# Matmul with layer norm: row pieces of A laid out for contiguous transposes, and a last row tile in six column ranges

## The chip, the cores and the metric

The kernel runs on one core of a Trainium2 chip. The metric is the time of one execution on the device in microseconds (us). Eight runs of the kernel before gave a median of 252.48 us, from 251.8 to 254.12.

The core has five engines that run side by side[...]: TensorE (PE in the profile; its weight loads are PEld), VectorE (DVE), ScalarE (ACT), GpSimd (POOL) and SyncE (SP). SP, ACT and POOL also issue transfers between memory (HBM) and the on-chip memory SBUF. TensorE writes its products to PSUM, eight banks of 512 fp32 columns on 128 partitions.

## The reference

```python
x = np.matmul(a, b)                         # a, b: 2048 x 2048, fp32
mean = np.mean(x, axis=-1, keepdims=True)
var = np.var(x, axis=-1, keepdims=True)
normalized = (x - mean) / np.sqrt(var + eps)
return (gamma * normalized + beta).astype(np.float32)
```

A product of two square matrices, and each row of it normalised to mean 0 and variance 1, scaled by gamma and shifted by beta. The inputs are cast to fp16 for the product; sums, statistics and output are fp32.

## The kernel before

**Tiles.** The 2048 rows of the output are 16 row tiles of 128. A row tile's 2048 columns are four banks of 512 (`bank`, L128), and each bank is the sum of 16 matmuls over the inner dimension (`mm`, L131). B stays on the chip in fp16 as `b16`, 16 slices of 128 inner rows. `b_rows` (L65) deals the inner index as `(c p t)` with t = 4, so that slice 4c + t holds inner index 512 c + 4 p + t on partition p; A's transposes use the same order.

**First four row tiles.** They run while B is still loading (L233 to L362): rows of A come in 16 pieces (`load_first`), VectorE casts them, TensorE turns them (`turn_first`, L99), VectorE keeps them (`keep_first`). Their products are made in two halves of the inner dimension, the first half put aside by ScalarE (`put_by`) and added later by VectorE (`add_up`).

**Later row tiles, 4 to 15.** Each comes in two halves h of the inner dimension. `load_tile` (L108) issues four transfers for a half, one for each group of 32 partitions; SP issues those of tiles 4 and 5, POOL those of tiles 6 to 15, into four buffers ("first"). In `a_pieces` (L66) partition r of group q holds rows 4 r + j, j = 0 to 3, of the row tile, for columns 512 c + 128 q to + 127. ScalarE casts a half (`cast_tile`, L114), 1024 elements a partition. VectorE then turns 32 x 32 blocks (`transpose_part`, L122): one call takes one j, all four c, 512 elements a partition; it reads inner index k in steps of 4 elements and writes rows r into `at` in steps of 4 elements.

**Order.** The engines' orders are those of the program text (L215 to L219): every engine executes its instructions in the order in which the Python code emits them, and the framework adds the semaphores. The loop over row tiles 4 to 15 (L370) emits for tile i: the normalisation of tile i - 1 (`normalise`, L179), then for each bank its 16 matmuls, its statistics on VectorE (`stats`, L137) and, up to i = 13, a cast and a transpose for tile i + 2. For i from 4 to 11 half a normalisation of one of the first four tiles follows as well (L384).

**Normalising.** `aggregate` (L151) joins four statistics into mean and variance on VectorE and takes the square root of variance + eps on ScalarE; `invert` (L159) is VectorE's reciprocal. Each bank is centred and multiplied by gamma (`centre`, L164, which reads PSUM and so frees the bank), then multiplied by the reciprocal and added to beta (`scale`, L170). SP sends out halves of 1024 columns.

**The last row tile** has its own normalisation (`normalise_last`, L194): after the last bank's statistics VectorE does three of the banks, each centred and scaled, and ScalarE and POOL do the fourth; four output transfers of 512 columns follow, three from SP and one from ScalarE's queue.

Of the kernel before, what the change touches and what calls it, by code (L numbers as in the profile page):

```python
# [9 lines left out]
FP32 = mybir.dt.float32  # L10
FP16 = mybir.dt.float16
AluOp = mybir.AluOpType
ActFn = mybir.ActivationFunctionType

@with_exitstack
def kernel(
# [18 lines left out]
    nc = tc.nc  # L35
    P = 128
    M, K = a.shape
    _, N = b.shape
    n_mt = M // P
    n_kt = K // P  # L40
    NB = 512
    n_nb = N // NB
    NH = N // 2
    G = 4

    konst = ctx.enter_context(tc.tile_pool(name="konst", bufs=1))
    bpool = ctx.enter_context(tc.tile_pool(name="bpool", bufs=1))
    bigp = ctx.enter_context(tc.tile_pool(name="bigp", bufs=8))
    firstp = ctx.enter_context(tc.tile_pool(name="firstp", bufs=4))
# [3 lines left out]
    xpool = ctx.enter_context(tc.tile_pool(name="xpool", bufs=16))  # L53
    upool = ctx.enter_context(tc.tile_pool(name="upool", bufs=2))
    stat = ctx.enter_context(tc.tile_pool(name="stat", bufs=6))
    psum = ctx.enter_context(tc.tile_pool(name="psum", bufs=1, space=bass.MemoryType.PSUM))

    gamma_b = konst.tile([P, N], FP32)
    beta_b = konst.tile([P, N], FP32)
    eps_t = konst.tile([P, 1], FP32)  # L60
    warm = konst.tile([P, NB], FP16)
    ident = konst.tile([P, P], FP16)
    b16 = bpool.tile([P, n_kt, N], FP16)

    b_rows = b.rearrange("(c p t) n -> c t p n", p=P, t=4)  # L65
    a_pieces = a.rearrange("(i r j) (c q k) -> q i r (j c) k", r=32, j=4, c=4, q=4)  # L66

    bnst, x_of, mv_of, rs_of, at = {}, {}, {}, {}, {}
    a_in, b_in, t_of, tile_in, part = {}, {}, {}, {}, {}
# [36 lines left out]
        nc.vector.tensor_copy(at[g][:, ds(4 * c, 4), :], t_of[n])  # L106

    def load_tile(i, h, queue):  # L108
        f = firstp.tile([P, 8, P], FP32, tag="first", name=f"p{i}_{h}")
        for q in range(4):  # L110
            queue.dma_start(f[ds(32 * q, 32)], a_pieces[q, i][:, ds(8 * h, 8)])  # L111
        tile_in[i, h] = f

    def cast_tile(i, h):  # L114
        a16 = a16p.tile([P, 2, 4, P], FP16, tag="a16", name=f"a{i}_{h}")
        nc.scalar.copy(a16.rearrange("p j c k -> p (j c) k"), tile_in.pop((i, h)))  # L116
        tile_in[i, h] = a16

    def new_at(i):
        at[i] = atp.tile([P, n_kt, P], FP16, tag="at", name=f"at{i}")  # L120

    def transpose_part(i, j):  # L122
        nc.vector.transpose(  # L123
            at[i].rearrange("p ct (r j) -> p j ct r", j=4)[:, j],
            tile_in[i, j // 2][:, j % 2].rearrange("p c (k t) -> p c t k", t=4),
        )

    def bank(i, q):  # L128
        x_of[i, q] = psum.tile([P, NB], FP32, tag="c_ps", bufs=8, name=f"ps_{i}_{q}")

    def mm(i, q, kt, lo=0, hi=n_kt):  # L131
        nc.tensor.matmul(  # L132
            x_of[i, q], at[i][:, kt, :], b16[:, kt, ds(q * NB, NB)],
            start=(kt == lo), stop=(kt == hi - 1),
        )

    def stats(i, q):  # L137
        if i not in bnst:
            bnst[i] = stat.tile([P, n_nb, 6], FP32, tag="bnst", name=f"bnst{i}")
        nc.vector.bn_stats(bnst[i][:, q, :], x_of[i, q])  # L140
# [10 lines left out]
    def aggregate(i):  # L151
        mv = stat.tile([P, 2], FP32, tag="mv", name=f"mv{i}")
        nc.vector.bn_aggr(mv, bnst[i])  # L153
        sq = stat.tile([P, 1], FP32, tag="sq", name=f"sq{i}")
        nc.scalar.activation(sq, mv[:, 1:2], ActFn.Sqrt, bias=eps_t)  # L155
        mv_of[i] = mv
        return sq

    def invert(i, sq):  # L159
        rs = stat.tile([P, 1], FP32, tag="rs", name=f"rs{i}")  # L160
        nc.vector.reciprocal(rs, sq)  # L161
        rs_of[i] = rs

    def centre(i, q, u):  # L164
        nc.vector.scalar_tensor_tensor(  # L165
            u, x_of[i, q], mv_of[i][:, 0:1], gamma_b[:, ds(q * NB, NB)],
            AluOp.subtract, AluOp.mult,
        )

    def scale(i, q, u, c):  # L170
        nc.vector.scalar_tensor_tensor(  # L171
            c[:, ds(q % 2 * NB, NB)], u, rs_of[i], beta_b[:, ds(q * NB, NB)],
            AluOp.mult, AluOp.add,
        )

    def new_c(i, h):
        return bigp.tile([P, NH], FP32, tag="big", name=f"c{i}_{h}")

    def normalise(i, h=None):  # L179
        if h in (None, 0):  # L180
            sq = aggregate(i)
        for half in (0, 1) if h is None else (h,):
            c = new_c(i, half)
            us = []
            for q in (2 * half, 2 * half + 1):
                us.append(upool.tile([P, NB], FP32, tag="u", name=f"u_{i}_{q}"))
                centre(i, q, us[-1])
                if q == 0:
                    invert(i, sq)
            for q in (2 * half, 2 * half + 1):  # L190
                scale(i, q, us[q % 2], c)
            nc.sync.dma_start(out[ts(i, P), ds(half * NH, NH)], c)

    def normalise_last(i):  # L194
        sq = aggregate(i)
        c = [new_c(i, 0), new_c(i, 1)]
        centre(i, 0, x_of[i, 0])
        invert(i, sq)
        shift = stat.tile([P, 1], FP32, tag="shift", name="shift")
        nc.vector.scalar_tensor_tensor(  # L200
            shift, mv_of[i][:, 0:1], -1.0, rs_of[i], AluOp.mult, AluOp.mult)
        q3 = ds(3 * NB, NB)
        y = upool.tile([P, NB], FP32, tag="u", name="y_last")
        nc.scalar.activation(y, x_of[i, 3], ActFn.Identity, bias=shift, scale=rs_of[i])  # L204
        nc.gpsimd.tensor_tensor(y, y, gamma_b[:, q3], AluOp.mult)  # L205
        nc.gpsimd.tensor_tensor(c[1][:, NB:NH], y, beta_b[:, q3], AluOp.add)
        for q in range(3):
            if q:
                centre(i, q, x_of[i, q])
            scale(i, q, x_of[i, q], c[q // 2])  # L210
            nc.sync.dma_start(
                out[ts(i, P), ds(q * NB, NB)], c[q // 2][:, ds(q % 2 * NB, NB)])
        nc.scalar.dma_start(out[ts(i, P), q3], c[1][:, NB:NH])

    order = {  # L215
        mybir.EngineType.PE, mybir.EngineType.DVE, mybir.EngineType.Activation,
# [2 lines left out]
    with tc.manual_schedule(engines=order):  # L219
# [5 lines left out]
        def warm_up(n):  # L225
# [4 lines left out]
            out=ident, in_=ident, compare_op=AluOp.not_equal, fill=1.0,  # L230
# [17 lines left out]
        for i in (4, 5):  # L248
            for h in (0, 1):
                load_tile(i, h, nc.sync)  # L250
        nc.sync.dma_start(gamma_b, gamma.unsqueeze(0).to_broadcast([P, N]))
        nc.sync.dma_start(beta_b, beta.unsqueeze(0).to_broadcast([P, N]))
        for i in range(6, n_mt):
            for h in (0, 1):
                load_tile(i, h, nc.gpsimd)
# [13 lines left out]
        for n in range(KH):  # L269
            g, c = pieces[n]  # L270
# [34 lines left out]
        for t in range(KH):  # L305
            n = KH + t
# [47 lines left out]
        for h in (0, 1):  # L354
            cast_tile(4, h)
            transpose_part(4, 2 * h)
            transpose_part(4, 2 * h + 1)
# [7 lines left out]
        for c in range(4):  # L365
            if c % 2 == 0:
                cast_tile(5, c // 2)
            transpose_part(5, c)

        for i in range(G, n_mt):  # L370
            if i > G:
                normalise(i - 1)
            if i + 2 < n_mt:
                new_at(i + 2)
            for q in range(n_nb):
                bank(i, q)
                for t in range(n_kt):
                    mm(i, q, t)
                stats(i, q)
                if i + 2 < n_mt:  # L380
                    if q % 2 == 0:
                        cast_tile(i + 2, q // 2)
                    transpose_part(i + 2, q)
                if q == 3 and i < 3 * G:  # L384
                    normalise((i - G) // 2, (i - G) % 2)
        normalise_last(n_mt - 1)

_INS = ['a', 'b', 'gamma', 'beta', 'eps']
_OUTS = [((2048, 2048), 'float32')]
# [28 lines left out]
```

## Time and profile before

| | us |
|---|---|
| median of 8 runs | 252.48 |
| the profiled execution | 252.12 |
| its span, first to last instruction | 250.3 |
| TensorE busy | 233.7 (93%) |
| VectorE busy | 213.9 (85%) |
| ScalarE busy | 58.4 (23%) |
| POOL busy | 49.2 (20%) |
| transposes on VectorE (L123), 48 | 61.4 |
| POOL's transfers of A (L111), 80 of 128 KB | 46.2 |
| TensorE waiting for centring (L165) | 3.6 |

The span is the time between the first and last instruction that the profiler saw; the execution takes a little longer. A group's duration counts from an instruction's start to its end, and neighbouring instructions of one engine overlap by some of it, so that the distance between two starts is the better price of one more instruction in a row. In a line of the order of time the first number is the start, the second the length of the merged stretch, xN the number of instructions in it, and the bracket, where there is one, is how long the engine had been idle and what ended this.

### The profile page before, as it was taken

Reading aid. Unit: us, or ns where it says so; the run is one execution under the profiler, and the core shown is the slowest. Engines: PE = TensorE matmul, PEld = TensorE weight load, DVE = VectorE, ACT = ScalarE, POOL = GpSimd, SP = SyncE. Lnnn points to the kernel's source line nnn. Section 1 sums busy time; section 2 is a strip of 40 time slices with the busy share of each in tenths; the row PEclk is TensorE's granted clock in tenths of the full one; section 3 lists DMA queues with packets and bytes.
Section 4 is the critical chain, followed back from the end, with each engine's and each line's share of the span. In section 5 each row is a group of like instructions: output and inputs, shape, how many; then the busy total and the mean of one; then the engine's idle time right before and its main releaser. Section 6 shows DMA issues by size and latency. Waiting matters only on the chain.

```text
span 250.3 us, 3093 instructions
## 1 busy us (share of the span) xinstructions
PE 233.7 (93%) x1108; PEld 106.4 (42%) x1108; DVE 213.9 (85%) x354; ACT 58.4 (23%) x91; POOL 49.2 (20%) x87
## 2 busy tenths in 40 slices
PE   7999999999999999999999999989979899999940
PEld 2444454444444444444444444434434344444410
DVE  1654454379999999999999999999999999999953
ACT  2225728641511321030300303011030303000010
POOL 0000000000732907051160702407042000000003
PEclk9999999999999999999999999999999999999996
DMA  5999999999999837458272762908448240404214
GB/s 183 404 394 403 402 401 408 408 367 169 226 283 230 208 91 235 147 191 230 86 233 102 239 180 106 310 25 230 169 153 264 90 168 3 168 0 168 115 53 168
DMA packets 20302, 52.62 MB, mean 210 GB/s; under 512 B 2880, under 2 KB 6976, under 8 KB 20032
## 3 DMA queue, kind: packets, MB, share of 16 engines
q1 hardware_dynamic: 16160, 41.16, 45.9%
q0 software_dynamic: 3840, 10.49, 16.9%
q10 hardware_dynamic: 288, 0.79, 0.9%
q8 instruction: 8, 0.13, 0.3%
q14 instruction: 6, 0.05, 0.1%
HBM read 35.65 MB, written 16.78 MB: 209 GB/s over the span
## 4 chain that ended last, share of the span: by engine, by line
DVE 56%; PE 28%; DMA 8%; issue 3%; ACT 2%; SPq 0%; DVEq 0%
PE ps L132 27%; DVE at L123 19%; DVE c L171 12%; DVE u L165 10%; DVE bnst L140 9%; DMA f<-in_a_dram 5%; DMA w<-in_b_dram 3%; DVE x L148 2%; ACT x L144 2%; DVE ps L165 1%; PE t_ps L102 1%; DVE mv L153 1%; ACT b L84 1%; DVE b L83 1%; DVE rs L161 1%
## 5 line engine op out<-in xcount | busy, mean ns | idle before, releaser
L132 PE MATMUL ps<-b,at 128*128 128x512 f16 x1024 | 224.4, 379 | 4.0 <-DVE u L165 3.6
L132 PEld LDWEIGHTS <-at 128*128 128x128 f16 x1024 | 99.7, 98 | 123.3 <-issue 5.9
L111 POOL DMA_DIRECT2D p<-in_a_dram x80 | 46.2, 585 | 141.7 <-DMA p<-in_a_dram 70.5
L123 DVE STREAM_TRANSPOSE at<-a 128x512 f16<-128x512 f16 x48 | 61.4, 1303 | 0.0
L171 DVE SCALAR_TENSOR_TENSOR c<-u,rs,beta_b 128x512 f32<-128x512 f32 x60 | 42.1, 744 | 0.0
L155 ACT ACTIVATE sq<-mv,eps_t 128x1 f32<-128x1 f32 x16 | 4.7, 295 | 136.2 <-DVE mv L153 136.2
L140 DVE BATCH_NORM_STATS2 bnst<-ps 128x6 f32<-128x512 f32 x48 | 30.9, 653 | 2.4 <-PE ps L132 2.4
L165 DVE SCALAR_TENSOR_TENSOR u<-ps,mv,gamma_b 128x512 f32<-128x512 f32 x44 | 31.6, 742 | 0.4
L116 ACT CAST a<-p 128x1024 f16<-128x1024 f32 x24 | 24.1, 1037 | 15.5 <-DMA p<-in_a_dram 15.5
L96 DVE CAST h<-f 128x512 f16<-128x512 f32 x16 | 6.8, 423 | 9.3 <-DMA f<-in_a_dram 9.3
L78 DVE CAST b<-w 128x512 f16<-128x512 f32 x16 | 6.7, 425 | 9.2 <-DMA w<-in_b_dram 9.2
L79 ACT CAST b<-w 128x512 f16<-128x512 f32 x16 | 9.6, 619 | 17.2 <-DMA w<-in_b_dram 17.2
L84 ACT CAST b<-w 128x512 f16<-128x512 f32 x16 | 10.0, 624 | 14.3 <-DMA w<-in_b_dram 14.3
L148 DVE TENSOR_TENSOR x<-ps,x 128x512 f32<-128x512 f32 x16 | 10.4, 683 | 3.1 <-PE ps L132 2.9
L205 POOL TENSOR_TENSOR y_last<-y_last,gamma_b 128x512 f32<-128x512 f32 x1 | 1.3, 1260 | 54.2 <-ACT y_last L204 54.2
L165 DVE SCALAR_TENSOR_TENSOR u<-x,mv,gamma_b 128x512 f32<-128x512 f32 x16 | 11.3, 727 | 0.2
L106 DVE COPY at<-t_ps 128x512 f16<-128x512 f16 x16 | 6.7, 421 | 4.7 <-PE t_ps L102 4.6
L140 DVE BATCH_NORM_STATS2 bnst<-x 128x6 f32<-128x512 f32 x16 | 10.0, 679 | 0.0
L227 PE MATMUL w_ps<-warm 128*128 128x512 f16 x20 | 7.4, 514 | 1.2 <-DVE warm L220 1.2
L144 ACT COPY x<-ps 128x512 f32<-128x512 f32 x16 | 8.4, 611 | 0.1
L83 DVE CAST b<-w 128x512 f16<-128x512 f32 x16 | 6.7, 417 | 2.0 <-DMA w<-in_b_dram 2.0
L102 PEld LDWEIGHTS <-h 128*128 128x128 f16 x64 | 5.3, 115 | 6.9 <-DVE h L96 2.8
(19 smaller groups left out, 25.3 us busy)
## 6 DMA issues: line engine op xcount, KB each, us to landing
w<-in_b_dram SPq DMA_DIRECT2D x31, 512.0 KB, 8.5
out_dram<-c SPq DMA_DIRECT2D x30, 512.0 KB, 2.7
p<-in_a_dram POOLq DMA_DIRECT2D x80, 128.0 KB, 5.4
f<-in_a_dram SPq DMA_DIRECT2D x16, 256.0 KB, 7.2
p<-in_a_dram SPq DMA_DIRECT2D x16, 128.0 KB, 5.2
gamma_b<-in_gamma_dram SPq DMA_DIRECT2D x1, 1024.0 KB, 10.0
beta_b<-in_beta_dram SPq DMA_DIRECT2D x1, 1024.0 KB, 14.9
out_dram<-c SPq DMA_DIRECT2D x3, 256.0 KB, 2.5
```

The source lines that it names most:

```text
L79: nc.scalar.copy(b16[:, kt, NB:NH], w[:, NB:NH])
L83: nc.vector.tensor_copy(b16[:, kt, NH:NH + NB], w[:, 0:NB])
L84: nc.scalar.copy(b16[:, kt, NH + NB:N], w[:, NB:NH])
L111: queue.dma_start(f[ds(32 * q, 32)], a_pieces[q, i][:, ds(8 * h, 8)])
L116: nc.scalar.copy(a16.rearrange("p j c k -> p (j c) k"), tile_in.pop((i, h)))
L123: nc.vector.transpose(at[i].rearrange("p ct (r j) -> p j ct r", j=4)[:, j], tile_in[i, j // 2][:, j % 2].rearrange("p c (k t) -> p c t k", ...
L132: nc.tensor.matmul(x_of[i, q], at[i][:, kt, :], b16[:, kt, ds(q * NB, NB)], start=(kt == lo), stop=(kt == hi - 1),)
L140: nc.vector.bn_stats(bnst[i][:, q, :], x_of[i, q])
L144: nc.scalar.copy(part[i, q], x_of[i, q])
L148: nc.vector.tensor_tensor(x, x_of[i, q], x, AluOp.add)
L165: nc.vector.scalar_tensor_tensor(u, x_of[i, q], mv_of[i][:, 0:1], gamma_b[:, ds(q * NB, NB)], AluOp.subtract, AluOp.mult,)
L171: nc.vector.scalar_tensor_tensor(c[:, ds(q % 2 * NB, NB)], u, rs_of[i], beta_b[:, ds(q * NB, NB)], AluOp.mult, AluOp.add,)
```

## The change

**Layout of tiles 4 to 15.** Partition r of a group now holds rows r, 32 + r, 64 + r and 96 + r of the row tile (32 s + r, with s = 0 to 3). A half's transfers are issued for one c at a time: eight of 64 KB, each of 32 partitions x 4 rows x 512 bytes, in place of four of 128 KB. One call of `transpose_part` now takes one c and all four j; it reads as before in steps of 4 elements and writes rows r of `at` next to each other.

**Mean of the last row tile by a matmul.** `b16` grows by 32 columns. In tiles 6 to 13 ScalarE sums every half row of B (`sum_b`, 32 calls of 1024 elements, the copy itself going to `junk`). After tile 14's matmuls and statistics, `mean_b` makes from these the mean of each row of B on VectorE, splits it into two fp16 parts, and ScalarE copies them into columns 2048 and 2049 of each of the 16 slices. The first column range of tile 15 includes them, and so its product holds the mean of each output row in two parts (`mean_last`).

**Six column ranges.** Tile 15's columns are made in the order 1760 to 2047 (with the two extra columns 290 wide), 1472 to 1759, 960 to 1471, 448 to 959, 128 to 447 and 0 to 127, with statistics after each and centring after each of the first four. `finish_last` centres the fifth while ScalarE takes the square root, centres the sixth on ScalarE and multiplies it by gamma on POOL, and then scales: four ranges on VectorE, two on ScalarE with POOL adding beta. Six output transfers follow, four from SP and two from ScalarE's queue.

```diff
-    b16 = bpool.tile([P, n_kt, N], FP16)
+    b16 = bpool.tile([P, n_kt, N + 32], FP16)
...
-    a_pieces = a.rearrange("(i r j) (c q k) -> q i r (j c) k", r=32, j=4, c=4, q=4)
+    a_pieces = a.rearrange("(s r) (c q k) -> q c r s k", r=32, c=4, q=4)
...
     def load_tile(i, h, queue):
-        f = firstp.tile([P, 8, P], FP32, tag="first", name=f"p{i}_{h}")
-        for q in range(4):
-            queue.dma_start(f[ds(32 * q, 32)], a_pieces[q, i][:, ds(8 * h, 8)])
+        f = firstp.tile([P, 2, 4, P], FP32, tag="first", name=f"p{i}_{h}")
+        for c in (0, 1):
+            for q in range(4):
+                queue.dma_start(
+                    f[ds(32 * q, 32), c], a_pieces[q, 2 * h + c][:, ds(4 * i, 4)])
...
-    def transpose_part(i, j):
+    def transpose_part(i, c):
         nc.vector.transpose(
-            at[i].rearrange("p ct (r j) -> p j ct r", j=4)[:, j],
-            tile_in[i, j // 2][:, j % 2].rearrange("p c (k t) -> p c t k", t=4),
+            at[i][:, ds(4 * c, 4), :].rearrange("p t (j r) -> p j t r", r=32),
+            tile_in[i, c // 2][:, c % 2].rearrange("p j (k t) -> p j t k", t=4),
         )
...
+    spans = [(1760, 290), (1472, 288), (960, 512), (448, 512), (128, 320), (0, 128)]
...
+    def sum_b(j, junk):
+        kt, h = j // 2, j % 2
+        nc.scalar.activation(
+            junk, b16[:, kt, ds(h * NH, NH)], ActFn.Copy, accum_out=b_sum[:, h, kt:kt + 1])
+
+    def mean_b():
+        nc.vector.tensor_tensor(b_mean, b_sum[:, 0, :], b_sum[:, 1, :], AluOp.add)
+        nc.vector.tensor_scalar(b_mean, b_mean, 1.0 / N, None, AluOp.mult)
+        nc.vector.tensor_copy(b_hilo[:, :, 0], b_mean)
+        nc.vector.tensor_tensor(b_hilo[:, :, 1], b_mean, b_hilo[:, :, 0], AluOp.subtract)
+        for kt in range(n_kt):
+            nc.scalar.copy(b16[:, kt, N:N + 2], b_hilo[:, kt, :])
+
+    def products_last(j):
+        lo, w = spans[j]
+        x = psum.tile([P, NB], FP32, tag="c_ps", bufs=8, name=f"ps_last_{j}")
+        for t in range(n_kt):
+            nc.tensor.matmul(
+                x[:, 0:w], at[last][:, t, :], b16[:, t, ds(lo, w)],
+                start=(t == 0), stop=(t == n_kt - 1))
+        x_of[last, j] = x
+
+    def mean_last():
+        w = N - spans[0][0]
+        parts = stat.tile([P, 2], FP32, tag="mv", name="mean_parts")
+        nc.vector.tensor_copy(parts, x_of[last, 0][:, w:w + 2])
+        m = konst.tile([P, 2], FP32)
+        nc.vector.tensor_tensor(m[:, 0:1], parts[:, 0:1], parts[:, 1:2], AluOp.add)
+        nc.vector.tensor_scalar(m[:, 1:2], m[:, 0:1], -1.0, None, AluOp.mult)
+        mv_of[last] = m
...
+    def finish_last():
...
+        nc.scalar.activation(y, x_of[i, n][:, 0:w], ActFn.Identity, bias=mv_of[i][:, 1:2])
+        nc.gpsimd.tensor_tensor(y, y, gamma_b[:, ds(lo, w)], AluOp.mult)
+        u_last[n] = y
+        mv = stat.tile([P, 2], FP32, tag="mv", name="mv_last")
+        nc.vector.bn_aggr(mv, bnst[i])
+        sq = stat.tile([P, 1], FP32, tag="sq", name="sq_last")
+        nc.scalar.activation(sq, mv[:, 1:2], ActFn.Sqrt, bias=eps_t)
+        centre_last(n - 1)
         invert(i, sq)
...
+        for j in (n, 0):
+            lo, w = spans[j]
+            u, o = u_last[j], homes[j]
+            nc.scalar.activation(u, u, ActFn.Copy, scale=rs)
+            nc.gpsimd.tensor_tensor(o, u, beta_b[:, ds(lo, o.shape[1])], AluOp.add)
+        for j in (3, 2, 1, 4):
+            lo, w = spans[j]
+            nc.vector.scalar_tensor_tensor(
+                homes[j], u_last[j], rs, beta_b[:, ds(lo, w)], AluOp.mult, AluOp.add)
+        for j in (3, n, 2, 0, 1, 4):
+            o = homes[j]
+            queue = nc.scalar if j in (n, 0) else nc.sync
+            queue.dma_start(out[ts(i, P), ds(spans[j][0], o.shape[1])], o)
...
-        for i in range(G, n_mt):
+        for i in range(G, last):
+            if i == 6:
+                junk = xpool.tile([P, 2 * NB], FP16, tag="x_sb", name="junk")
             if i > G:
                 normalise(i - 1)
...
+                if 6 <= i < 14:
+                    sum_b(4 * (i - 6) + q, junk)
                 if q == 3 and i < 3 * G:
                     normalise((i - G) // 2, (i - G) % 2)
-        normalise_last(n_mt - 1)
+        mean_b()
+        normalise(last - 1)
+        for j in range(len(spans)):
+            products_last(j)
+            if j == 0:
+                mean_last()
+            stats_last(j)
+            if j < len(spans) - 2:
+                centre_last(j)
+        finish_last()
```

More of the change, by code (lines that the diff above doesn't have):

```diff
@@ L62 @@
     ident = konst.tile([P, P], FP16)
-    b16 = bpool.tile([P, n_kt, N], FP16)
+    b16 = bpool.tile([P, n_kt, N + 32], FP16)
+    b_sum = konst.tile([P, 2, n_kt], FP32)
+    b_mean = konst.tile([P, n_kt], FP32)
+    b_hilo = konst.tile([P, n_kt, 2], FP16)
     b_rows = b.rearrange("(c p t) n -> c t p n", p=P, t=4)
-    a_pieces = a.rearrange("(i r j) (c q k) -> q i r (j c) k", r=32, j=4, c=4, q=4)
+    a_pieces = a.rearrange("(s r) (c q k) -> q c r s k", r=32, c=4, q=4)
     bnst, x_of, mv_of, rs_of, at = {}, {}, {}, {}, {}
@@ L115, in cast_tile @@
         a16 = a16p.tile([P, 2, 4, P], FP16, tag="a16", name=f"a{i}_{h}")
-        nc.scalar.copy(a16.rearrange("p j c k -> p (j c) k"), tile_in.pop((i, h)))
+        nc.scalar.copy(a16, tile_in.pop((i, h)))
         tile_in[i, h] = a16
@@ L192, in normalise @@
             nc.sync.dma_start(out[ts(i, P), ds(half * NH, NH)], c)
[L194 to L197, printed above, removed]
-        invert(i, sq)
[L199 to L213, printed above, removed]
+    spans = [(1760, 290), (1472, 288), (960, 512), (448, 512), (128, 320), (0, 128)]
@@ new lines @@
+    last = n_mt - 1
+    u_last = {}
+    def sum_b(j, junk):
[9 more added lines that the diff above has]
+            nc.scalar.copy(b16[:, kt, N:N + 2], b_hilo[:, kt, :])
@@ new lines, in stats_last, with centre_last @@
+    def stats_last(j):
+        if j == 0:
+            bnst[last] = stat.tile([P, len(spans), 6], FP32, tag="bnst_last", bufs=1,
+                                   name="bnst_last")
+        lo, w = spans[j]
+        nc.vector.bn_stats(bnst[last][:, j, :], x_of[last, j][:, 0:min(w, N - lo)])
+    def centre_last(j):
+        lo, w = spans[j]
+        w = min(w, N - lo)
+        x = x_of[last, j][:, 0:w]
+        if j == 0:
+            u = upool.tile([P, NB], FP32, tag="u", name="u_last_0")[:, 0:w]
+        else:
+            u = x
+        nc.vector.scalar_tensor_tensor(
+            u, x, mv_of[last][:, 0:1], gamma_b[:, ds(lo, w)], AluOp.subtract, AluOp.mult)
+        u_last[j] = u
@@ new lines, in finish_last @@
+    def finish_last():
+        i, n = last, len(spans) - 1
+        c = {0: new_c(i, 0), 1: new_c(i, 1)}
+        lo, w = spans[n]
+        y = upool.tile([P, NB], FP32, tag="u", name="u_last_n")[:, 0:w]
+        nc.scalar.activation(y, x_of[i, n][:, 0:w], ActFn.Identity, bias=mv_of[i][:, 1:2])
[6 more added lines that the diff above has]
+        centre_last(n - 1)
+        invert(i, sq)
+        rs = rs_of[i]
+        homes = {3: c[0][:, 0:512], 2: c[0][:, 512:1024], 1: c[1][:, 0:288],
+                 4: c[1][:, 288:608], n: c[1][:, 608:736], 0: c[1][:, 736:1024]}
+        for j in (n, 0):
+            lo, w = spans[j]
+            u, o = u_last[j], homes[j]
+            nc.scalar.activation(u, u, ActFn.Copy, scale=rs)
+            nc.gpsimd.tensor_tensor(o, u, beta_b[:, ds(lo, o.shape[1])], AluOp.add)
+        for j in (3, 2, 1, 4):
+            lo, w = spans[j]
+            nc.vector.scalar_tensor_tensor(
+                homes[j], u_last[j], rs, beta_b[:, ds(lo, w)], AluOp.mult, AluOp.add)
[3 more added lines that the diff above has]
+            queue.dma_start(out[ts(i, P), ds(spans[j][0], o.shape[1])], o)
@@ L383 @@
                     transpose_part(i + 2, q)
+                if 6 <= i < 14:
+                    sum_b(4 * (i - 6) + q, junk)
                 if q == 3 and i < 3 * G:
                     normalise((i - G) // 2, (i - G) % 2)
-        normalise_last(n_mt - 1)
+        mean_b()
+        normalise(last - 1)
+        for j in range(len(spans)):
+            products_last(j)
+            if j == 0:
+                mean_last()
[3 more added lines that the diff above has]
+        finish_last()
 _INS = ['a', 'b', 'gamma', 'beta', 'eps']
```

## The prediction

> **What bounds the kernel now.** I read the groups first, then TensorE's order of time, VectorE's, and the tail. The groups (line, engine, operation, count | busy us, mean ns | idle before, releaser):
>
> ```profile
> L132 PE MATMUL ps<-b,at 128*128 128x512 f16 x1024 | 224.4, 379 | 4.0 <-DVE u L165 3.6
> ...
> L123 DVE STREAM_TRANSPOSE at<-a 128x512 f16<-128x512 f16 x48 | 61.4, 1303 | 0.0
> ```
>
> TensorE waits for VectorE 3.6 us in all, at centring (L165), which frees PSUM banks. Where, by TensorE's order of time:
>
> ```profile
> 59.79 93.83 PE L132 MATMUL ps<-b,at 128*128 128x512 f16 x434
> 153.91 13.97 PE L132 MATMUL ps<-b,at 128*128 128x512 f16 x64 [0.29 <-DVE u L165]
> 168.85 13.97 PE L132 MATMUL ps<-b,at 128*128 128x512 f16 x64 [0.96 <-DVE u L165]
> 184.16 13.97 PE L132 MATMUL ps<-b,at 128*128 128x512 f16 x64 [1.35 <-DVE u L165]
> 199.11 41.60 PE L132 MATMUL ps<-b,at 128*128 128x512 f16 x192 [0.97 <-DVE u L165]
> ```
>
> 434 matmuls in 93.83 us are 216.2 ns each, 13.85 us for a row tile of 64. Only the four bracketed waits, 0.29 + 0.96 + 1.35 + 0.97 = 3.57 us, stand between this and an unbroken TensorE. VectorE in the same stretch:
>
> ```profile
> 98.59 1.30 DVE L123 STREAM_TRANSPOSE at<-a 128x512 f16<-128x512 f16 x1
> 99.71 0.63 DVE L140 BATCH_NORM_STATS2 bnst<-ps 128x6 f32<-128x512 f32 x1
> 100.26 1.29 DVE L123 STREAM_TRANSPOSE at<-a 128x512 f16<-128x512 f16 x1
> ...
> 228.26 2.48 DVE L140 BATCH_NORM_STATS2 bnst<-ps 128x6 f32<-128x512 f32 x4
> 230.77 0.26 DVE L153 BATCH_NORM_AGGREGATE mv<-bnst 128x2 f32<-128x24 f32 x1
> ```
>
> From start to start a transpose takes 1.11 us, statistics 0.55. Two tiles of tiles 4 to 11 (aggregation at 122.58 to the same at 152.82) take VectorE 30.24 us, 15.1 each, against TensorE's 13.85: VectorE falls behind until the banks run out. It still is behind at tile 14's end: TensorE finished it at 240.75 - 13.85 = 226.9, VectorE's statistics of it end at 230.77. Then the tail:
>
> ```profile
> 240.75 0.70 DVE L140 BATCH_NORM_STATS2 bnst<-ps 128x6 f32<-128x512 f32 x1 [2.44 <-PE ps L132]
> 241.48 0.26 DVE L153 BATCH_NORM_AGGREGATE mv<-bnst 128x2 f32<-128x24 f32 x1
> ...
> 242.44 0.15 DVE L161 RECIPROCAL rs<-sq 128x1 f32<-128x1 f32 x1
> ...
> 245.61 0.75 DVE L171 SCALAR_TENSOR_TENSOR c<-ps,rs,beta_b 128x512 f32<-128x512 f32 x1
> ...
> 246.39 0.33 SPq L211 DMA_DIRECT2D out_dram<-c  x1
> ```
>
> The last matmul ends at 240.75, the last scaling at 246.36, the span at 250.3: 9.55 us of tail, of which the last output transfer and the end take 3.94.
>
> [...] It steps 8 bytes on both sides: read (k in steps of 4 halves) and write (r in steps of 4). [...] casts of 1024 take 1037 ns, and two take 1.98 us.
>
> **Part 1, the layout.** Only the transposes' write side becomes contiguous; the read step stays. What speaks for the write side being the slow one is a strided read elsewhere in this trace, TensorE's first-tile turns, whose weights are read in 8-byte steps (h[:, :, t]):
>
> ```profile
> 30.15 0.39 PE L102 MATMUL t_ps<-ident,h 128*128 128x128 f16 x4
> 30.37 1.67 PE L132 MATMUL ps<-b,at 128*128 128x512 f16 x7
> ```
>
> Four of them start within 0.22 us, 55 ns for a load of 128 strided halves, far above VectorE's rate. That is another engine's port, so it is evidence, not proof. Bounds for one transpose: [...] 1.11 (nothing gained). I take 0.58.
>
> What a saving d is worth: VectorE is 230.77 - 0.70 = 230.07 at the start of tile 14's last statistics; TensorE without its four waits would be at 226.9 - 3.57 = 223.3. So 6.8 us over 48 transposes, d = 0.14 us, removes all there is; 0.58 gives 0.53. More than 0.14 buys only cover: tiles 4 to 11 then take VectorE 15.1 - 4 x 0.53 = 13.0 us, under 13.85. **Gain 3.57 us**, everything else being TensorE at its rate.
>
> The transfers double: 16 a tile on POOL, each 32 partitions x 4 x 512 B. At today's 0.585 us each (the cost for twice the bytes, so an upper bound) that is 9.4 us of a 13.85 us stage, and POOL has nothing else; the buffers freed by tile i+2's casts are filled for tile i+4, two stages ahead. Hidden, at nothing. SP's 16 issues for tiles 4 and 5 become 32, 16 x 0.31 = 5 us more, ahead of gamma and beta (issued at 65.5 and 66.2, landed 10.0 and 14.9 us later; beta is first wanted near 85). Least cover: tile 4's second half, cast at 65.01, wanted transposed by TensorE at 59.79 + 50 matmuls = 70.6. Before, its transposes were done at 68.8. Two transposes at 0.58 leave some 3 us for a late landing.
>
> **Part 2, the mean.** 32 sums on ScalarE at 0.95 us apart, four a stage for tiles 6 to 13: 3.8 us against 10 to 12.8 us of idle a stage (it waits for aggregation, 136 us in all). In its queue they stand behind the square root and between the casts: second cast done 4 us after the square root, its transposes wanted 7 us after. Nothing; were the cover gone, a late square root holds VectorE's reciprocal by up to 0.95 each.
>
> mean_b is different: its four VectorE steps stand behind tile 14's last statistics, and 16 ScalarE copies behind them fill the two columns that tile 15's first range reads. With T the end of tile 14 on TensorE: statistics to T+0.7; four dependent steps at 0.19 (reciprocal 242.44 to shift 242.63) to T+1.5; first copy [...] at T+1.75[...]. TensorE waits **1.8 us**. [...] Queued behind the copies is tile 14's square root: VectorE's reciprocal waits until T+3.5, normalise(14) ends near T+8.3.
>
> **Part 3, the ranges.** 2050 columns and 96 matmuls for 2048 and 64: [...] 13.95 us, **+0.1**; the 128-wide ones at the 55 ns seen above don't wait for weights. TensorE ends at T+15.75. VectorE, from T+8.3, does mean, statistics and centring of ranges 0 to 3 by T+14, range 4's statistics at T+14.9 to 15.3: no backlog. Then statistics of 128 columns (0.3), aggregation (0.27), square root (0.29) under range 4's centring (0.55), reciprocal to T+17.1, four scalings from T+17.15 at 0.66, 0.66, 0.43 and 0.55: T+19.4. Before, the same path was 5.6 us from the last matmul, now 3.65. ScalarE and POOL do the 128 and 288 columns: two ACT scalings to T+17.9, POOL's additions (1.26 us for 512, so 0.35 and 0.7) to T+18.7, before VectorE's. Last transfer and end 3.8 (160 KB for 256 KB; 3.94 at most). Tail 3.65 + 3.8 = 7.45 for 9.55: **2.1 us gained**.
>
> **Sum.** -3.57 + 1.8 + 0.1 - 2.1 = -3.8 us: span 246.5. The profiled execution took 252.12, 1.82 over its span, and the median of the runs is 252.48, 0.36 above it: 246.5 + 1.82 + 0.36 = 248.7 us.
>
> **Rivals.**
> - *The read side is the slow one; transposes stay at 1.11.* Then VectorE reaches tile 14's last statistics at 230.07 as before, and mean_b, queued behind that backlog, makes TensorE wait from 226.9 to 231.9 at the tile 14/15 boundary. End 230.07 + 23.2 = 253.3, median 255.4: slower. For it: the read step is untouched. Against: strided reads at TensorE. It decides at d = 0.06 us: 227.1 + 23.2 = 250.3, the old span.
> - *Partly faster, d = 0.03 to 0.1.* Span 251.8 to 248.5, median 254 to 250.7.
> - *The smaller transfers arrive late.* [...] After eight issues POOL now waits for an earlier landing before each next one (70.5 to 81.7), so half the size halves what is in flight. Tile 4 past its 3 us, by 2 us: 250.7. Against: in the steady stages 1 MB in 13.85 us, 76 GB/s, is enough.
>
> **How the numbers follow.** Forecast 0.70 (own range 247.3 to 250.2: copies 1.1 dearer, tail and end by half a microsecond each way), read side 0.20 (254.8 to 256), partly 0.05, late 0.05. 0.3% of the median is 0.76 us, about what a measurement can tell. Faster: 0.70, most of late and a third of partly, 0.74; slower 0.21; same 0.05. Range 247.3 to 255.0: it leaves out some of the forecast's ends (0.05) and most of the read side (0.13).
>
> **What would show it.** Transposes near 0.75 us in duration (1.30 less 0.53); no wait of TensorE for L165; instead one wait near 1.8 us for a copy into b at the start of tile 15, with VectorE waiting there for TensorE, not behind it; then under 7.7 us from last matmul to end. Transposes at 1.3 and a 5 us wait there make me wrong, as do casts that wait for p after 90 us.

## The result, and the profile after

The changed kernel takes 248.71 us (median of 11 runs, 248.35 to 250.25) against a median of 252.41 before; the ratio is estimated at 0.986, 95% interval 0.984 to 0.988. That is faster, and where it was forecast. The forecast span was 246.5 us, though, and the profiled execution's is 247.4; the two sections that follow say where the 0.9 us is. It didn't show in the median, because the profiled execution of the changed kernel (249.37 us) lies 0.66 us above the median of its runs, and the one before 0.36 below: that the medians agree to 0.01 us is luck.

The groups of the changed kernel, columns as before:

```profile
L137 PE MATMUL ps<-b,at 128*128 128x512 f16 x960 | 210.6, 379 | 0.8 <-DVE at L109 0.3
...
L208 ACT ACTIVATE junk<-b 128x1024 f16<-128x1024 f16 x32 | 33.7, 1054 | 0.5
L128 DVE STREAM_TRANSPOSE at<-a 128x512 f16<-128x512 f16 x48 | 32.6, 687 | 0.4 <-ACT a L121 0.4
```

A transpose lasts 687 ns where it lasted 1303. TensorE's order of time:

```profile
38.26 185.04 PE L137 MATMUL ps<-b,at 128*128 128x512 f16 x854
225.03 14.07 PE L223 MATMUL ps_last<-b,at 128*128 128x290 f16 x96 [1.73 <-ACT b L217]
```

From 38 us to the end of tile 14 there is no wait for centring: all four are gone. In their place stands one, 1.73 us ahead of tile 15, for ScalarE's copies into b. All engines around it, in order of time (lines left out between):

```profile
223.34 0.70 DVE L145 BATCH_NORM_STATS2 bnst<-ps 128x6 f32<-128x512 f32 x1 [2.75 <-PE ps L137]
223.96 0.16 DVE L212 TENSOR_TENSOR b_mean<-b_sum 128x16 f32<-128x16 f32 x1
...
224.57 0.18 DVE L215 TENSOR_TENSOR b_hilo<-b_mean,b_hilo 128x16 f16<-128x16 f32 x1
...
224.79 1.59 ACT L217 COPY b<-b_hilo 128x2 f16<-128x2 f16 x16 [13.47 <-DVE b_hilo L215]
...
226.29 0.29 ACT L160 ACTIVATE sq<-mv,eps_t 128x1 f32<-128x1 f32 x1
226.61 0.16 DVE L166 RECIPROCAL rs<-sq 128x1 f32<-128x1 f32 x1 [0.90 <-ACT sq L160]
```

VectorE now waits 2.75 us for TensorE at tile 14's end, where it had been 3.9 us behind. Then comes the chain as it was laid out: statistics, four steps, the first copy; the square root behind the 16 copies, and VectorE's reciprocal behind the square root. The tail:

```profile
239.14 0.30 DVE L242 BATCH_NORM_STATS2 bnst_last<-ps_last 128x6 f32<-128x128 f32 x1 [0.40 <-PE ps_last L223]
...
240.35 2.29 DVE L280 SCALAR_TENSOR_TENSOR c<-ps_last,rs,beta_b 128x512 f32<-128x512 f32 x4
...
241.13 2.00 SPq L285 DMA_DIRECT2D out_dram<-c  x4
241.31 0.80 POOL L277 TENSOR_TENSOR c<-u_last,beta_b 128x288 f32<-128x288 f32 x1
```

The last matmul ends at 239.10. The last scaling ends 3.5 us after it (5.6 before), but the span goes on for 4.76 us more (3.94 before).

### The profile page after: what moved, and what is told of

It reads as the page before. It is cut to its first block, busy times and chain, and to the rows that moved or that the text cites. A ratio compares the mean times of both kernels' runs of the same rounds, so it can differ in the third digit from the quotient of the medians.

```text
span 247.4 us, 3406 instructions
## 1 busy us (share of the span) xinstructions
PE 233.2 (94%) x1140; PEld 108.8 (44%) x1140; DVE 194.7 (79%) x365; ACT 96.0 (39%) x173; POOL 89.0 (36%) x168
## 4 chain that ended last, share of the span: by engine, by line
PE 78%; DMA 16%; ACT 2%; DVE 2%; DVEq 0%; issue 0%; SPq 0%
PE ps L137 72%; DMA w<-in_b_dram 11%; PE ps_last L223 6%; DMA f<-in_a_dram 5%; ACT x L149 2%; DVE c L280 1%; DVE bnst L145 0%; DVEq L498 0%; ACT b L82 0%; DVE h L99 0%; DVE ps_last L252 0%; SPq L94 0%; DVE mv_last L265 0%; DVE bnst_last L242 0%; ACT b L217 0%
## 5 line engine op out<-in xcount | busy, mean ns | idle before, releaser
L137 PE MATMUL ps<-b,at 128*128 128x512 f16 x960 | 210.6, 379 | 0.8 <-DVE at L109 0.3
L137 PEld LDWEIGHTS <-at 128*128 128x128 f16 x960 | 93.5, 98 | 112.2 <-issue 2.2
L115 POOL DMA_DIRECT2D p<-in_a_dram x160 | 86.9, 550 | 95.5 <-DVE bnst L145 61.4
L145 DVE BATCH_NORM_STATS2 bnst<-ps 128x6 f32<-128x512 f32 x44 | 29.8, 679 | 13.1 <-PE ps L137 13.1
L208 ACT ACTIVATE junk<-b 128x1024 f16<-128x1024 f16 x32 | 33.7, 1054 | 0.5
L128 DVE STREAM_TRANSPOSE at<-a 128x512 f16<-128x512 f16 x48 | 32.6, 687 | 0.4 <-ACT a L121 0.4
L121 ACT CAST a<-p 128x1024 f16<-128x1024 f32 x24 | 24.7, 1039 | 14.2 <-DMA p<-in_a_dram 14.1
L262 POOL TENSOR_TENSOR u_last_n<-u_last_n,gamma_b 128x128 f32<-128x128 f32 x1 | 0.5, 452 | 56.0 <-ACT u_last_n L261 56.0
L223 PE MATMUL ps_last<-b,at 128*128 128x512 f16 (+4 forms) x96 | 14.1, 308 | 1.7 <-ACT b L217 1.7
L223 PEld LDWEIGHTS <-at 128*128 128x128 f16 x96 | 8.8, 98 | 7.3 <-issue 2.0
```

The source lines that it names most:

```text
L115: queue.dma_start(f[ds(32 * q, 32), c], a_pieces[q, 2 * h + c][:, ds(4 * i, 4)])
L121: nc.scalar.copy(a16, tile_in.pop((i, h)))
L128: nc.vector.transpose(at[i][:, ds(4 * c, 4), :].rearrange("p t (j r) -> p j t r", r=32), tile_in[i, c // 2][:, c % 2].rearrange("p j (k t) ...
L137: nc.tensor.matmul(x_of[i, q], at[i][:, kt, :], b16[:, kt, ds(q * NB, NB)], start=(kt == lo), stop=(kt == hi - 1),)
L208: nc.scalar.activation(junk, b16[:, kt, ds(h * NH, NH)], ActFn.Copy, accum_out=b_sum[:, h, kt:kt + 1])
L223: nc.tensor.matmul(x[:, 0:w], at[last][:, t, :], b16[:, t, ds(lo, w)], start=(t == 0), stop=(t == n_kt - 1))
```

## The experiments

**The layout alone.** The kernel before with the new `a_pieces`, `load_tile` and `transpose_part`.

> The kernel before with the layout of tiles 4 to 15 alone (64 KB transfers, contiguous transpose writes), the last row tile as before. Theory (layout gives the whole 3.57 us of TensorE's waits; the new last row tile gives 2.1 back and takes 1.8 + 0.1): last matmul at 240.75 - 3.57 = 237.2, tail 9.55 as before, span 246.7, about 248.8 us, within 0.5 us of the full change. Rival (the gain is shared, the last row tile earns its part): 250 to 251 us, clearly slower than the full change.

Measured: 249.73 us, ratio to before 0.990 (0.986 to 0.994); span 247.2. No wait of TensorE for centring; from the last matmul (statistics start at 236.32) to the end 10.9 us, 1.3 more than in the kernel before, with the same instructions in it. It fits neither forecast: it is 1.0 us above the full change, where the theory allowed 0.5, and below the rival's 250. So the layout carries most of the gain; its interval and the full change's overlap, and what the new last row tile adds on top is not told apart by these times. In the traces, from the start of tile 14's last statistics to the end takes 24.7 us here (222.51 to 247.2) and 24.1 in the changed kernel (223.34 to 247.4): some 0.6 us, where the terms of the forecast leave 0.2 (2.1 less 1.8 and 0.1).

**The new last row tile alone.** Layout, transfers and transposes as before.

> The kernel before with the new last row tile alone (sums, mean, six ranges), layout and transfers of A as before. Theory (the mean's four steps queue behind VectorE's backlog, TensorE waits at the start of tile 15): a wait of about 5 us there, VectorE's last statistics of tile 14 near 230.1 and 24.1 us from there to the end (as measured in the changed kernel): span 254.2, 255.5 to 256.2 us. Rival (the ranges are worth their shorter tail whatever the layout): about 251 us.

Measured: 258.53 us, ratio 1.023 (1.020 to 1.026), slower than either forecast. TensorE's order of time, and its stretches by window (core's columns: PE, PEld, DVE, ACT and POOL busy, then the granted TensorE clock, DMA share, GB/s):

```profile
198.69 27.79 PE L135 MATMUL ps<-b,at 128*128 128x512 f16 x128 [0.95 <-DVE u L168]
231.29 16.23 PE L221 MATMUL ps_last<-b,at 128*128 128x290 f16 x96 [4.82 <-ACT b L215]
```

```profile
226.45:231.29 4.84, 0.03 (x1) 0.00 (x0) 4.70 (x13) 0.24 (x3) 0.00 (x0) 0.75 0.46 186
231.29:247.50 16.21, 16.21 (x96) 9.67 (x95) 10.64 (x21) 1.55 (x16) 0.00 (x0) 0.86 0.17 66
```

The wait of about 5 us is there (4.82), at the place and for the reason given: without the faster transposes, mean_b stands behind VectorE's backlog. What I had not counted is that the wait makes what follows it slower: the clock granted to TensorE falls, and tile 15 takes 16.23 us where it takes 14.07 in the changed kernel. The 0.86 is a mean: the 16 matmuls of the first range took 4.0 us where they take 2.1 in the changed kernel, those of the second 2.4 for 2.1, and those of the other four as long as there (7.1, 2.3 and 1.1 us for 512, 320 and 128 columns). At half the clock that would be the tile's first 4.5 us, an estimate from the 0.86 over 16.21 us. In the other five executions, 258.3 to 259.3 us, the mean clock of the whole was lower (0.976 or 0.977) than in the profiled one (257.0 us, 0.982), so the clock may cost more in them.

**Filling that wait.** The same kernel with matmuls on zeros in the gap:

```diff
         normalise(last - 1)
+        w_ps = psum.tile([P, NB], FP32, tag="c_ps", bufs=8, name="w_ps_late")
+        warm_up(20)
         for j in range(len(spans)):
```

> The ranges alone on the old layout (as ranges_only), with 20 matmuls of 128x512 on zeros put between tiles 14 and 15, whose product nobody reads: they fill the wait of 4.82 us. Theory (the 290- and 288-wide matmuls after the wait ran at a lowered clock, 16.23 us for the tile instead of 14.07, because TensorE had stood still for 4.8 us): granted clock 1.00 in tile 15, the tile in 14.1 us, about 2.1 us less than ranges_only: 256.4 us. Rival (the matmuls of tile 15 are slow from waits on the copies or on banks): tile 15 still 16.2 us, the time as ranges_only.

```profile
226.00:231.50 5.50, 5.40 (x26) 2.35 (x24) 5.40 (x12) 0.00 (x0) 0.00 (x0) 1.00 0.47 191
231.50:246.00 14.50, 14.07 (x96) 8.70 (x95) 10.92 (x23) 1.79 (x17) 0.00 (x0) 1.00 0.19 73
```

Clock 1.00, tile 15 in 14.07 us, 255.45 us in all (1.009, 1.006 to 1.012): 3.1 us less than without the useless work. The slow matmuls came from the standstill. With this the read-side rival's price is accounted for: its 255.4 us is the time of the ranges on slow transposes (here with the old transfers) without the clock's part.

**Which step of a transpose costs.** Each row tile with its own steps:

```diff
+        rd, wr = ((1, 1), (4, 1), (1, 4), (4, 4), (2, 1), (1, 2), (8, 1), (1, 8),
+                  (16, 1), (1, 16), (2, 2), (8, 8))[i - 4]
         nc.vector.transpose(
-            at[i][:, ds(4 * c, 4), :].rearrange("p t (j r) -> p j t r", r=32),
-            tile_in[i, c // 2][:, c % 2].rearrange("p j (k t) -> p j t k", t=4),
+            at[i][:, ds(4 * c, 4), :].rearrange("p t m -> p (t m)").rearrange(
+                "p (o r s) -> p o s r", r=32, s=wr),
+            tile_in[i, c // 2][:, c % 2].rearrange("p j m -> p (j m)").rearrange(
+                "p (o k s) -> p o s k", k=32, s=rd),
         )
```

> The changed kernel, each row tile's transposes with another pair of steps, in fp16 elements, for reading and writing (which makes the product of tiles 4 to 15 that of shuffled operands, the amount of work the same): tile 4 (1,1), 5 (4,1), 6 (1,4), 7 (4,4), 8 (2,1), 9 (1,2), 10 (8,1), 11 (1,8), 12 (16,1), 13 (1,16), 14 (2,2), 15 (8,8). Theory (only the write step costs): (4,1) as (1,1), 0.69 us; (1,4) as (4,4), 1.30 us. Rival (either strided side is free alone, both together cost): (1,4) at 0.69 us. Steps of 8 and 16 are open: a read step could start to cost there.

VectorE's order of time, in the order of the pairs read/write (1,1), (4,1), (1,4), (4,4), (2,1), (1,2), (8,1), (1,8), (16,1), (1,16); the first line merges two transposes, the second four:

```profile
63.92 1.29 DVE L130 STREAM_TRANSPOSE at<-a 128x512 f16<-128x512 f16 x2
...
77.27 2.48 DVE L130 STREAM_TRANSPOSE at<-a 128x512 f16<-128x512 f16 x4
...
81.91 1.31 DVE L130 STREAM_TRANSPOSE at<-a 128x512 f16<-128x512 f16 x1
...
97.22 1.29 DVE L130 STREAM_TRANSPOSE at<-a 128x512 f16<-128x512 f16 x1
...
111.69 0.69 DVE L130 STREAM_TRANSPOSE at<-a 128x512 f16<-128x512 f16 x1
...
125.12 0.72 DVE L130 STREAM_TRANSPOSE at<-a 128x512 f16<-128x512 f16 x1
...
138.59 1.09 DVE L130 STREAM_TRANSPOSE at<-a 128x512 f16<-128x512 f16 x1
...
154.61 2.43 DVE L130 STREAM_TRANSPOSE at<-a 128x512 f16<-128x512 f16 x1
...
172.52 1.08 DVE L130 STREAM_TRANSPOSE at<-a 128x512 f16<-128x512 f16 x1
...
188.45 2.32 DVE L130 STREAM_TRANSPOSE at<-a 128x512 f16<-128x512 f16 x1
```

This settles the main point. A read step of 4 halves with contiguous writes runs as fast as no step at all (2.48 us for four and 1.29 for two, 0.6 from start to start in both); a write step of 4 with contiguous reads is as slow as both together (1.31 and 1.29). A write step of 2 costs almost nothing (0.72), 8 takes 3.5 times as long (2.43). Reads cost with a step of 8 (1.09). It is one execution, but the four transposes of each pair agree within 0.05 us. So the change took away the only strided side that cost.

**The smaller transfers alone.** The kernel before, each of A's later transfers cut in two.

```diff
-            queue.dma_start(f[ds(32 * q, 32)], a_pieces[q, i][:, ds(8 * h, 8)])
+            for j in (0, 1):
+                queue.dma_start(
+                    f[ds(32 * q, 32), ds(4 * j, 4)], a_pieces[q, i][:, ds(8 * h + 4 * j, 4)])
```

> The kernel before with the transfers of tiles 4 to 15 cut in two (64 KB each, same addresses, same strided transposes). Theory (twice the issues are hidden): the time of before within 0.3%. Rival (late landings of tiles 4 to 6 hold VectorE): 1 to 2 us slower.

Measured: 254.06 us, ratio 1.007 (1.004 to 1.010): 1.5 us slower, so "at nothing" was wrong. But not by late landings, as the rival had it: TensorE's waits are the same four, 0.30, 0.97, 1.34 and 0.98. The profiled execution (255.17 us, 1.1 above the median) is 1.8 us late at its last matmul, but it has lost this by 46 us, before the first of these transfers is issued at 50.6. From the last matmul to the end it takes 10.8 us, where the kernel before takes 9.55: 1.2 us of the 1.5, in the close of the kernel, after the last output. The closing drain of POOL's and SP's queues (duration min/median/max ns, first and last start), in the kernel before:

```profile
L413 POOLq DRAIN  x3: 40/102/3592, 245.0 to 250.1; - x3
L413 SPq DRAIN  x3: 7/7/7, 249.5 to 249.8; - x3
```

and with the layout alone:

```profile
L415 POOLq DRAIN  x3: 40/102/5798, 240.6 to 246.9; - x3
L415 SPq DRAIN  x3: 7/7/7, 245.2 to 246.6; - x3
```

SP's first drain comes 0.2 to 0.3 us after the last output has landed, and stands for the landing here. POOL's long one starts with its last operation. Before, it ended at 245.0 + 3.6 = 248.6, ahead of the landing (249.5), and the span ended 0.8 after the landing. With the layout alone it ends at 240.6 + 5.8 = 246.4, 1.2 us behind the landing (245.2), and the span ends 0.8 after the drain. With the cut transfers it is the same: 246.8 + 5.8 = 252.6, the landing at 251.4. Measured from the end of POOL's last operation, the drain takes 2.3 us with 80 transfers of 128 KB and 4.5 with 160 of 64 KB. In the changed kernel it ends at 246.6, the landing is at 246.0: 0.6 us of the end.

**Few contiguous tiles.** The changed kernel, tiles 7 to 15 writing in steps of 4 halves again.

```diff
+        form = "p t (j r) -> p j t r" if i < 7 else "p t (r j) -> p j t r"
         nc.vector.transpose(
-            at[i][:, ds(4 * c, 4), :].rearrange("p t (j r) -> p j t r", r=32),
+            at[i][:, ds(4 * c, 4), :].rearrange(form, r=32),
```

> The changed kernel, but only tiles 4, 5 and 6 write their transposes contiguously; tiles 7 to 15 write in steps of 8 bytes as before (which leaves the rows of these tiles in another order in the output). Theory (6.8 us saved on VectorE are all that can be used): 12 transposes x 0.50 us = 6.0 us, so TensorE's waits are gone and VectorE is behind by some 0.8 us at tile 14's end: 0.5 to 1.5 us above the changed kernel. Rival (the gain goes with the number of faster transposes): a quarter of the way from the ranges alone, about 254 us.

Measured: 254.89 us, 1.009 (1.006 to 1.012): the theory falls. Six us were saved on VectorE, but at tile 14's end it was early by only some 3 (its statistics there start at 224.95 for 227.82 with the ranges alone), and TensorE had the full wait of 4.82 us and the slow tile 15. 2.3 us of what was saved went at once, into VectorE's waits for a cast and for TensorE, which it doesn't have with the ranges alone:

```profile
66.67 1.30 DVE L129 STREAM_TRANSPOSE at<-a 128x512 f16<-128x512 f16 x2 [1.06 <-ACT a L121]
84.84 0.70 DVE L146 BATCH_NORM_STATS2 bnst<-ps 128x6 f32<-128x512 f32 x1 [1.23 <-PE ps L138]
```

An engine that has caught up can save no more for later. My 0.14 us per transpose took every saving as kept, whenever it was made. The rival isn't shown either: by its rule, a quarter of the way from the 258.5 us that the ranges alone took, it would be 256.1.

**The mean earlier.** The four steps and 16 copies inside tile 14:

```diff
+                if i == last - 1 and q == 1:
+                    mean_b()
...
-        mean_b()
         normalise(last - 1)
```

> The changed kernel with the mean of B's rows made inside tile 14, after its second bank's statistics, instead of after tile 14. Theory (the 1.73 us wait of TensorE at tile 15 comes from these steps standing behind tile 14's last statistics): no wait there, the last matmul at 237.4, 1.7 us less: 247.0 us. Rival (something else, as the banks or VectorE's backlog, holds TensorE there): less than 0.5 us gained, or VectorE late in tile 15 and the end unmoved.

Measured: 246.80 us, 0.979 (0.975 to 0.982). Tile 15 follows tile 14 without a wait:

```profile
38.03 184.48 PE L137 MATMUL ps<-b,at 128*128 128x512 f16 x854
222.35 14.07 PE L223 MATMUL ps_last<-b,at 128*128 128x290 f16 x96
```

The 1.9 us less than the changed kernel fit the wait. Its bracket, 1.73, counts from the modelled end of the matmul before it, 0.38 us after that one's start; in an unbroken row the next one starts 0.22 us after it. So taking a wait away saves 0.16 us more than its bracket, here 1.89. For the four waits of the kernel before it makes 4.2 us, not 3.57, and that shows. There the same 854 matmuls, from the start of this line to the end of tile 14 at 226.9, take 188.7 us, waits and all:

```profile
38.21 115.42 PE L132 MATMUL ps<-b,at 128*128 128x512 f16 x534
```

Here they take 184.48.

**Four outputs for six.** The columns of the last tile laid so that four transfers send them.

```diff
...
-        for j in (3, n, 2, 0, 1, 4):
-            o = homes[j]
-            queue = nc.scalar if j in (n, 0) else nc.sync
-            queue.dma_start(out[ts(i, P), ds(spans[j][0], o.shape[1])], o)
+        nc.sync.dma_start(out[ts(i, P), ds(448, 512)], homes[3])
+        nc.sync.dma_start(out[ts(i, P), ds(960, 512)], homes[2])
+        nc.scalar.dma_start(out[ts(i, P), ds(1472, 576)], c[1][:, 448:1024])
+        nc.sync.dma_start(out[ts(i, P), ds(0, 448)], c[1][:, 0:448])
...
```

> As mean_early, and the last row tile's output in four transfers (512, 512, 576 and 448 columns) instead of six. From the last scaling to the end the changed kernel took 4.76 us where 3.94 were taken before and 3.8 forecast. Theory A (the six transfers with their issues crowd each other): back to about 4.0 us, 0.7 us less than mean_early. Theory B (it is the chip's spread from run to run, or the short rows): within 0.2 us of mean_early.

Measured: 246.91 us, 0.977 (0.975 to 0.980): as mean_early, and so is the stretch from the last range's statistics to the end, 8.2 us in both. POOL's drain holds the end in both, so the time alone wouldn't show an earlier landing; but the landing came no earlier either, 3.5 us after the last scaling for 3.4. The number of outputs isn't what lengthens the end.

**What sets POOL's drain.** Three kernels with other queues for A's transfers, on top of mean_early. Half, or all, of those of tiles 8 to 15 from ScalarE's queue:

```diff
-        for i in range(6, n_mt):
+        for i in (6, 7):
...
                         cast_tile(i + 2, q // 2)
+                        if i + 4 < n_mt:
+                            load_tile(i + 4, q // 2, nc.scalar if q else nc.gpsimd)
```

> As mean_early, with half of the transfers of tiles 8 to 15 issued from ScalarE's queue, each right after the cast that frees its buffer: POOL issues 96 transfers instead of 160. Theory (POOL's closing drain grows with the transfers that it issued: 2.3 us after its last operation with 80, 4.54 with 160, so 0.0275 us each and 0.13 fixed): 2.8 us with 96; the drain then ends before the last output lands, and the span ends 0.8 us after the landing as before: 0.6 us less than mean_early, 246.2 us. Rival (the drain's length comes from the size or layout of the transfers or from another part of the change): still about 4.5 us, time as mean_early.

Measured: 250.95 us, 0.992 (0.989 to 0.995), 4 us more than mean_early (3.4 by the two ratios), though tile 15 starts with no wait and VectorE's tail is the same. From the last range's statistics to the end takes 11.7 us (237.58 to 249.3), in mean_early 8.2, so the loss is in the close:

```profile
L501 POOLq DRAIN  x3: 40/102/8758, 239.7 to 249.0; - x3
L501 SPq DRAIN  x3: 7/7/7, 244.5 to 248.7; - x3
```

The outputs had landed by 244.5; POOL's drain lasts to 248.5, 8.0 us past its last operation, with fewer transfers. Theory and rival both fall, but that the drain can hold the end is shown.

> As early_split, but all transfers of tiles 8 to 15 from ScalarE's queue: POOL issues 32. Theory: POOL's drain 1.0 us after its last operation; no further gain, as the landing bounds the end already: 246.2 us, unless ScalarE, with 16 issues a tile at some 0.36 us each (5.8 us of 13.85, beside some 7 us of casts and sums), makes casts or square roots late and VectorE waits. Rival: drain 4.5 us, time as mean_early or above.

Measured: 261.49 us, 1.035 (1.031 to 1.038). The drain is 2.7 us with POOL's 32 transfers. The time is lost to the caution named in the expectation, only larger: eight issues in a row took ScalarE 3.70 us, 0.46 each where 0.36 was assumed.

```profile
150.61 3.70 ACTq L115 DMA_DIRECT2D p<-in_a_dram  x8
```

What stands behind them in ScalarE's order waits, and those who need it wait for ScalarE (who waited for whom, us in total, times, longest; in the first line ScalarE's own issues count as waiting):

```profile
ACT junk L208 <- DMA p<-in_a_dram: 44.3, 10, 6.0
...
DVE rs L166 <- ACT sq L160: 15.3, 7, 3.5
DVE at L128 <- ACT a L121: 13.1, 8, 5.1
...
PE ps L137 <- DVE u L170: 10.5, 4, 4.6
```

Last, tiles 6 and 7 from SP, which is idle then:

```diff
-                load_tile(i, h, nc.gpsimd)
+                load_tile(i, h, nc.sync if i < 8 else nc.gpsimd)
```

> As mean_early, with the transfers of tiles 6 and 7 issued by SP after gamma and beta, so that POOL issues 128. POOL's closing drain was 2.7 us after its last operation with 32 transfers, 8.0 with 96 (both without a pause of POOL in between), 4.5 with 160 and 2.3 with 80 of twice the size (both with one pause that nothing explains, 2.50 us before the 114th and 0.97 us before the 61st). Theory (POOL clears up 0.082 us for each transfer, part of it in one pause once some 105 of 64 KB are uncleared, the rest in the drain): 1.5 to 2.5 us of drain with 128, and the end bound by the landing: 0.6 us less than mean_early, 246.2 us. Rival (the drain only grows, and 160 was short for another reason): 10.5 us of drain, some 253 us.

```profile
L499 POOLq DRAIN  x3: 40/102/2715, 239.5 to 244.8; - x3
L499 SPq DRAIN  x3: 7/7/7, 244.2 to 244.5; - x3
```

Measured: 246.35 us, 0.976 (0.972 to 0.979), the lowest of all. The drain is 1.9 us from POOL's last operation, as the clearing theory said, and ends 2 us ahead of the landing; POOL's unexplained 2.50 us pause comes after 113 transfers, as in the changed kernel. From the last range's statistics to the end it takes 7.7 us (237.34 to 245.0), in mean_early 8.2 (236.46 to 244.7): 0.6 less, as forecast. The two medians differ by less than their intervals; the gain over mean_early is read from these lines. Per transfer the numbers agree: 96 and 32 transfers without a pause differ by 5.2 us, 0.082 each; 160 and 128 with a pause by 2.6, 0.082 each. What the pause clears, and why 80 larger transfers leave 2.3 us, stays open.

## Why the prediction was right, and where it wasn't

- **Layout, -3.57 us.** Right, with its reason. The write side was the slow one, which the sweep shows; a transpose's distance of 0.58 us was my estimate, which no trace of the kernel before showed, and is 0.6 in a row of them. Tile 14 ends at 223.3 on TensorE, as forecast, but that it fits so well is luck. The four waits were worth 4.2 us, not 3.57 (shown under *The mean earlier*), and the changed kernel's profiled execution lost 0.55 us of it between 44 and 46 us, while B was still arriving: 9 matmuls fall in this stretch, 11 in the traces of the kernel before and of mean_early. So its 854 matmuls take 185.04 us, those of mean_early 184.48.
- **Where 0.14 us per transpose would do.** The step failed in the few-tiles kernel: savings made while VectorE isn't behind are lost. At 0.5 us for every transpose the forecast didn't depend on it, but the point of decision of the first rival (0.06 us) rests on the same sum and was not tested.
- **Transfers, at nothing.** The step that failed. The cover in the stages was there (no cast waited for p after 78 us; tile 4's second half came late by 0.45 us for VectorE and not for TensorE, well within the 3 us). Nor did the rival's reading hold that half the size halves what is in flight: POOL now issues 16 in a row before it first waits for a landing, where it issued eight. The cost is at the end, where I had looked for none: POOL's drain, 1.2 us with the old last tile, 0.6 in the changed kernel.
- **Sums on ScalarE, at nothing.** Hidden, as said. Each also reads out its accumulator (187 ns), so they stand some 1.1 to 1.2 us apart, not 0.95.
- **The wait for the mean, 1.8 us.** 1.73. ScalarE's copies are 0.093 us apart (1.59 us for 16, 188 ns for one); what the forecast took for them was my estimate, which no trace of the kernel before showed. Moving the mean into tile 14 removes it.
- **Tile 15, 13.95 us.** 14.07; the forecast was my estimate.
- **The tail.** Last matmul to last scaling 3.65, measured 3.54. Last scaling to end forecast 3.8, measured 4.76: the term of the sum that was mis-sized. 0.6 us are POOL's drain; the other 0.3 or so are not settled: the landing came 3.4 us after the last scaling, 3.1 before, and four outputs instead of six didn't shorten it. So the last of the signs named, under 7.7 us from the last matmul to the end, failed: it is 8.3.
- **The rival on the other side.** Its mechanism and its wait (4.82 for 5) are shown by the ranges alone, its price was 3 us short: 2.2 us of it, in the profiled execution, is the clock after the standstill, which the forecast of the changed kernel, with a wait of 1.7 us at clock 1.00, didn't meet.

## What to carry to other kernels

Price a transpose on VectorE by its write pattern first: contiguous on the write side was worth half of its time here (687 ns for 1303), while the read side could keep its step of 4. Before moving a step that another engine waits for, look at what is queued in front of it: the same mean cost 4.8 us behind a backlog, 1.7 without it and nothing half a tile earlier. And count what a queue owes at the end of the kernel: transfers that are hidden all the way can come due in the close.

## What the runs showed of the hardware that I had not expected

- VectorE's transposes of fp16 (128x512) took 0.69 us with a read step of 2 halves and contiguous writes; write steps of 2, 4, 8 and 16 halves took 0.72, 1.30, 2.43 and 2.32 us. A read step of 4 cost nothing (2.48 us for four in a row, 0.6 from start to start), those of 8 and 16 made it 1.6 times as long (1.09 and 1.08 us).
- A standstill of TensorE of 1.7 us left its clock at 1.00, and the tile behind it took 14.07 us; after one of 4.8 us the clock was 0.86 over the tile, which took 16.23. With all later transfers on ScalarE, the 128 matmuls after a standstill of 4.60 us took 29.39 us, where 128 took 27.79 in the ranges alone.
- GpSimd's closing drain can hold the end of the kernel, after every output has landed. It grew by 0.082 us for each transfer of 64 KB that GpSimd had issued: 2.7 us after its last operation with 32 and 8.0 with 96, and, behind a pause of 2.5 us after the 113th, 1.9 with 128 and 4.5 with 160. That the pause clears some 105 of them is a reading that fits these four and isn't shown.
